# Output projections behind feed-forwards: the split of the last two inner tiles is issued one column tile earlier

## The chip, the cores and the metric

The kernel runs on one core of one Trainium2 chip. The metric is the device time of one execution in microseconds (us), here as the median over several runs.

## The reference, cut to what matters

The model is a two-layer decoder trunk on 256 tokens of width 1024. Each layer has a mixer (a short gated convolution in the first, an attention with three branches in the second) between two half-step feed-forwards, so that there are four feed-forwards in all:

```python
def swiglu_ffn(x, w_in, w_out):
    gate, up = jnp.split(x @ w_in, 2, axis=-1)
    return (jax.nn.silu(gate) * up) @ w_out
...
h = h + 0.5 * swiglu_ffn(rmsnorm(h, ffn1_norm[i]), ffn1_w_in[i], ffn1_w_out[i])
```

The inner width is 2816, which is 22 tiles of 128. The change concerns the last product, with `w_out`, of each of the four.

## The kernel before, in words

**Precision.** Every product is made of float32r matmuls on values that were split into a high half (a rounded copy) and a low half (what the rounding left). ScalarE (ACT) writes the high half, VectorE (DVE) subtracts to get the low half. For activations this is `split` (lines 361 to 363): one ACT cast on L362, then one DVE subtraction on L363, into one tile `act` of 128 x 512 whose left 256 columns are the high half and whose right 256 are the low half. A weight tile multiplies both halves with its own high part (128 x 512 matmuls, the function `wide`, L518), and its low part multiplies the high half alone (128 x 256 matmuls, the function `narrow`, L524).

**The weight stream.** `Stream` brings weights from HBM in blocks `ws` of 128 x 2048 (three buffers, issued on SyncE's queue, SP, L139). Half of a block is a unit: `high` casts it into `wh` on ACT (L166), `low` subtracts into `wl` on DVE (L183). At most six units are there at a time. When `narrow` has used the last tile of a unit, `W.done` lets the stream convert the unit that stands six further on. So the calls of `wide` and `narrow` also place casts on ACT's queue and subtractions on DVE's, in the order in which the program is written. Each engine works off its own instructions in that order; the order is not changed by a scheduler.

**The end of a feed-forward's first half.** `ffn_tokens` makes two inner tiles at a time. `turned` (L419) applies the SiLU and the gate and transposes, and sends the result to DRAM on SP (`turn`, L427); `placed` (L430) fetches it back in the layout that the output projection wants (`t<-turn`, L432); `halved` (L435) then calls `split` for the two tiles. For the last two inner tiles, `halved` is not called there but handed on as the function `rest`: two ACT casts and two DVE subtractions that are still to be issued.

**The output projection.** `out_proj` (L491) makes eight column tiles of 128 outputs. Each needs all 22 inner tiles. For the first four column tiles the work is cut in two. The first loop does inner tiles 0 to 17 of each of the four, 18 `wide` and then 18 `narrow` matmuls, in four PSUM banks. Then comes `rest()`. The second loop does inner tiles 18 to 21 of each of the four (four `wide`, four `narrow`) and hands the finished tile to `out_evac` (L473), which adds it to the residual on DVE (L475) and prepares the next norm. The weights of the first loop are nine units, 0 to 8; those of the second are units 9 and 10; column tiles five to eight follow from unit 11 on. In the first loop the third column tile uses up units 4 and 5, by which units 10 and 11 are converted; the fourth uses up units 6, 7 and 8, by which units 12, 13 and 14 are converted.

The calls with `rest` are the four behind feed-forwards: L702, L779, L1020 and L1362. The two other output projections, of the convolution and of the attention, don't take this way.

Of the kernel before, what the change touches and what calls it, by code (L numbers as in the profile page):

```python
# [69 lines left out]
def trunk(ctx, tc, A, out):  # L70
# [26 lines left out]
    def bank(shape=(P, 512)):  # L97
        return mk(shape, "a", 4, pool=ps)
# [250 lines left out]
    def a_pass(todo, last=7, mid=None):  # L349


        for o, u, xs, ks in todo:
            for k in ks:
                pe.matmul(o, u[0][:, k * P:(k + 1) * P], xs[k], start=(k == 0), stop=False)  # L354
        if mid is not None:
            mid()
        for o, u, xs, ks in todo:
            for k in ks:
                pe.matmul(o[:, :T], u[1][:, k * P:(k + 1) * P], xs[k][:, :T], start=False, stop=(k == last))  # L359
# [113 lines left out]
    def out_evac(o, c, factor, norm, short=False):  # L473
        for x in range(2):
            ve.scalar_tensor_tensor(out=h[c], in0=o[:, x * T:(x + 1) * T], scalar=factor, in1=h[c], op0=ALU.mult, op1=ALU.add)  # L475
        if not short:
            W.low()
            norm.tile(c)
            W.high()
            return  # L480
        norm.high(c)
        if c:
            norm.low(c - 1)
        if c < 5:
            W.low()
        W.high()
        norm.squares(c)
        if c == ND - 1:
            norm.low(c)

    def out_proj(lhs, factor, norm, final=False, rest=None):  # L491

        n, i, u = len(lhs), 0, None
        if rest is not None:
            n = NF
        head = []
        if n == 8:
            head = [(bank(), W.take()[0]) for _ in range(4)]
            cut = (7, 7, 7, 2)
            a_pass([(o, u, lhs, range(n)) for (o, u), n in zip(head, cut)])  # L500
        for c in range(len(head)):
            o, u = head[c]
            a_pass([(o, u, lhs, range(cut[c], 8))])
            W.done(1, False)
            out_evac(o, c, factor, norm, True)
        def tile():
            nonlocal i, u
            if i % 8 == 0:
                u, = W.take()
            q = slice(i % 8 * P, (i % 8 + 1) * P)  # L510
            i += 1
            return u[0][:, q], u[1][:, q], i % 8 == 0

        def wide(o, run, ks, last=None):
            for k in ks:
                while len(run) <= k:
                    run.append(tile())
                pe.matmul(o, run[k][0], lhs[k], start=(k == 0), stop=(k == last))  # L518

        def narrow(o, run, ks, last=None, free=True):  # L520
            for k in ks:
                while len(run) <= k:
                    run.append(tile())
                pe.matmul(o[:, :T], run[k][1], lhs[k][:, :T], start=False, stop=(k == last))  # L524
                if run[k][2] and free:
                    W.done(1, k < n - 1)

        c = len(head)
        if rest is not None:
            runs = [(bank(), []) for _ in range(4)]  # L530
            for o, run in runs:
                wide(o, run, range(n - 4))
                narrow(o, run, range(n - 4), n - 1)
            rest()
            for c, (o, run) in enumerate(runs):
                wide(o, run, range(n - 4, n))
                narrow(o, run, range(n - 4, n), n - 1)
                out_evac(o, c, factor, norm)
            c += 1
        while c < ND - final:  # L540
            o, run = bank(), []
            if n > 8 and c % 2 and c + 1 < ND - final:
                wide(o, run, range(n))
                o2, run2 = bank(), []
                wide(o2, run2, [0])
                narrow(o, run, range(n), n - 1)
                out_evac(o, c, factor, norm)
                narrow(o2, run2, range(n), free=False)
                wide(o2, run2, range(1, n), n - 1)
                for _ in range(sum(t[2] for t in run2)):  # L550
                    W.done(1, False)
                out_evac(o2, c + 1, factor, norm)
                W.pump()
                c += 2
                continue
            for ks in (range(n - 1), [n - 1]) if c == 0 else (range(n),):
                wide(o, run, ks)
                narrow(o, run, ks, n - 1)
            out_evac(o, c, factor, norm, n == 8)
            c += 1  # L560
        c -= 1
        if final:

            us = W.take((i + n + 7) // 8 - i // 8 - (i % 8 > 0))
            us = ([u] if i % 8 else []) + us
            w = [[us[(i % 8 + k) // 8][x][:, (i + k) % 8 * P:((i + k) % 8 + 1) * P] for x in range(2)] for k in range(n)]
            lo, hi = bank(), bank()
            for k in range(n):
                pe.matmul(lo[:, :T], w[k][0], lhs[k][:, T:], start=(k == 0), stop=(k == n - 1))
            ve.scalar_tensor_tensor(out=h[c + 1], in0=lo[:, :T], scalar=factor, in1=h[c + 1], op0=ALU.mult, op1=ALU.add)  # L570
            for q, o, ks in (slice(0, T), hi, range(n - 3)), (slice(0, P), hi, range(n - 3, n)), (slice(P, T), bank(), range(n - 3, n)):
                for k in ks:
                    pe.matmul(o[:, q], w[k][0], lhs[k][:, q], start=(k == ks[0] and q.start + k != n - 3), stop=False)
                    pe.matmul(o[:, q], w[k][1], lhs[k][:, q], start=False, stop=(k == n - 1))
                if k == n - 1:
                    z = q if o is not hi else slice(0, T)
                    ve.scalar_tensor_tensor(out=h[c + 1][:, z], in0=o[:, z], scalar=factor, in1=h[c + 1][:, z], op0=ALU.mult, op1=ALU.add)
                    norm.tile(c + 1, q)
        W.pump()
# [119 lines left out]
    hid, rest = ffn_tokens(xs, nm, n0=2, hid=hid, old=old)  # L699
    xs = new_xs()  # L700
    nm = Norm([(xs, G_MIX)])
    out_proj(hid, 0.5, nm, rest=rest)  # L702
    nm.halves()

# [40 lines left out]
    xs = new_xs()  # L745
    nm = Norm([(xs, G_FFN2)])
    out_proj(zs, 1.0, nm)
    bias = {}
    cbias = one([P, 8, 2, 2, 16], "cbias")
# [22 lines left out]
    hid, rest = ffn_tokens(xs, nm, bg=bias_bg, pre=lambda: list(tab))  # L772
# [4 lines left out]
    xkv = [xk_a[:, k] for k in range(4)] + [t2(dt=F32R) for _ in range(4)]  # L777
    nm = Norm([(xkv, G_KV), (xs, G_FFN1 + 8)])
    out_proj(hid, 0.5, nm, rest=rest)  # L779
    nm.halves()  # L780
    del hid
# [235 lines left out]
    hid, rest = ffn_tokens(xs, rc=rc, bg=bg)  # L1017
# [318 lines left out]
    for c in range(ND):  # L1336
        if c < 4:
            o = wo[c][0]
# [17 lines left out]
    hid, rest = ffn_tokens(xs, nm)  # L1356
# [93 lines left out]
```

## Time and profile before

| what | value |
|---|---|
| median of 3 runs | 964.2 us (963.87 to 965.33) |
| the profiled execution's own time | 964.24 us |
| its span in the trace | 962.5 us |
| busy: TensorE matmuls / weight loads | 951.4 us (99%) / 806.5 us (84%) |
| busy: VectorE / ScalarE / GpSimd | 662.3 / 538.7 / 136.5 us |
| granted TensorE clock | 1.00 |
| moved by DMA | 200.09 MB, 208 GB/s on the mean |

The span is what the trace covers, from the first to the last instruction; the execution's own time is 1.74 us longer. In rows of the trace, the number in front is the start in microseconds from the beginning of the span, the next one the duration; "x18" is a group of 18 instructions that follow each other, and the bracket behind a row is the idle time of the engine just before it and what ended that. The four output projections lie at about 127 to 190, 400 to 463, 623 to 687 and 896 to 957 us.

### The profile page before, as it was taken

How to read it: one execution, taken by the hardware profiler on the slowest of the kernel's cores; microseconds unless marked ns; L12 is line 12 of the kernel's file. 1: busy time of each engine (PE TensorE's matmuls, PEld its weight loads, DVE VectorE, ACT ScalarE, POOL GpSimd, SP SyncE). 2: the span in 40 equal slices, each digit the busy share in tenths (PEclk: the TensorE clock that was granted, in tenths of full speed). 3: DMA queues.
4: the chain of work that ended last, by engine and by line, in shares of the span. 5: the costliest groups of instructions: out<-in, count | busy, mean ns of one | idle time of the engine just before them, and what ended most of it. 6: DMA issues, size and time to landing. Idle time of an engine off the chain costs nothing.

```text
span 962.5 us, 13410 instructions
## 1 busy us (share of the span) xinstructions
PE 951.4 (99%) x4954; PEld 806.5 (84%) x4954; DVE 662.3 (69%) x1071; ACT 538.7 (56%) x903; POOL 136.5 (14%) x212
## 2 busy tenths in 40 slices
PE   9999999999999999999999999999999999999998
PEld 8888888888888888888888888888877888888888
DVE  6777667578896667656756676856579786677552
ACT  7755554455565555444647775644489774555430
POOL 2000000044520110001121031201137110000000
PEclk9999999999999999999999999999999999999999
DMA  8468885445546998764646886764511248877840
GB/s 308 176 219 264 277 258 191 190 176 208 179 170 242 262 280 259 229 239 175 218 163 206 266 254 239 250 240 161 197 46 46 89 175 267 277 221 243 276 160 21
DMA packets 127005, 200.09 MB, mean 208 GB/s; under 512 B 90539, under 2 KB 104875, under 8 KB 106332
## 3 DMA queue, kind: packets, MB, share of 16 engines
q1 hardware_dynamic: 126796, 198.97, 61.7%
q8 instruction: 39, 0.64, 0.3%
q10 hardware_dynamic: 144, 0.26, 0.1%
q14 instruction: 26, 0.21, 0.1%
HBM read 186.60 MB, written 12.09 MB: 206 GB/s over the span
## 4 chain that ended last, share of the span: by engine, by line
PE 98%; DVE 1%; DMA 1%; issue 0%; ACT 0%; SPq 0%; DVEq 0%
PE a L518 17%; PE mm L452 16%; PE mm L454 16%; PE mm L453 16%; PE a L524 9%; PE mm L354 4%; PE a L354 4%; PE mm L359 2%; PE a L359 2%; PE mm L1159 1%; PE mm L605 1%; PE a L1236 1%; PE a L795 1%; PE a L794 1%; PE a L796 1%; PE a L1204 1%
## 5 line engine op out<-in xcount | busy, mean ns | idle before, releaser
L183 DVE TENSOR_TENSOR wl<-ws,wh 128x1024 fp32r<-128x1024 f32 x318 | 390.5, 1253 | 191.8 <-ACT wh L166 155.0
L166 ACT CAST wh<-ws 128x1024 fp32r<-128x1024 f32 x318 | 325.9, 1047 | 190.7 <-DMA ws<-in_ffn_w_in_dram 84.9
L452 PE MATMUL mm<-wh,xs 128*128 128x512 f32 x672 | 262.6, 391 | 0.0
L454 PE MATMUL mm<-wl,xs 128*128 128x512 f32 x672 | 261.7, 389 | 0.0
L453 PE MATMUL mm<-wh,xs 128*128 128x512 f32 x672 | 261.5, 389 | 0.0
L518 PE MATMUL a<-act,wh 128*128 128x512 f32 x714 | 172.2, 392 | 6.4 <-DVE act L363 6.4
L518 PEld LDWEIGHTS a<-act,wh 128*128 128x128 f32 x714 | 131.2, 188 | 33.6 <-DVE act L363 8.3
L454 PEld LDWEIGHTS mm<-wl,xs 128*128 128x128 f32 x672 | 126.1, 188 | 27.0 <-DVE wl L183 0.5
L453 PEld LDWEIGHTS mm<-wh,xs 128*128 128x128 f32 x672 | 126.2, 188 | 25.7
L452 PEld LDWEIGHTS mm<-wh,xs 128*128 128x128 f32 x672 | 126.2, 188 | 25.7
L524 PEld LDWEIGHTS a<-act,wl 128*128 128x128 f32 x714 | 91.9, 191 | 3.6
L524 PE MATMUL a<-act,wl 128*128 128x256 f32 x714 | 93.0, 283 | 0.0
L315 POOL TENSOR_TENSOR sq<-sq,t 128x256 f32<-128x256 f32 x35 | 27.8, 795 | 382.8 <-ACT t L313 382.7
L423 ACT ACTIVATE t<-mm,rc 128x256 f32<-128x256 f32 x84 | 39.7, 473 | 56.6 <-DVE t L424 40.7
L298 ACT ACTIVATE xs<-base 128x256 fp32r<-128x256 f32 x48 | 24.0, 504 | 60.4 <-DVE base L475 50.7
L424 DVE SCALAR_TENSOR_TENSOR t<-mm,rc,t 128x256 f32<-128x256 f32 x84 | 40.5, 482 | 18.4 <-ACT t L423 15.2
L475 DVE SCALAR_TENSOR_TENSOR base<-a,base 128x256 f32<-128x256 f32 x78 | 32.8, 422 | 25.8 <-PE a L518 18.3
L362 ACT CAST act<-t 128x256 fp32r<-128x256 f32 x96 | 34.7, 404 | 24.8 <-DVE t L723 19.4
L363 DVE TENSOR_TENSOR act<-t,act 128x256 fp32r<-128x256 f32 x96 | 37.2, 424 | 5.9 <-ACT act L362 5.9
L425 DVE STREAM_TRANSPOSE t<-t 128x256 f32<-128x256 f32 x84 | 37.4, 446 | 3.0
L354 PE MATMUL mm<-xs,wh 128*128 128x512 f32 x144 | 34.7, 391 | 0.0
L302 DVE SCALAR_TENSOR_TENSOR xs<-base,xs 128x256 fp32r<-128x256 f32 x48 | 26.5, 556 | 9.5 <-ACT xs L298 9.4
(283 smaller groups left out, 900.5 us busy)
## 6 DMA issues: line engine op xcount, KB each, us to landing
ws<-in_ffn_w_in_dram SPq DMA_DIRECT2D x85, 1024.0 KB, 5.4
ws<-in_ffn_w_out_dram SPq DMA_DIRECT2D x44, 1024.0 KB, 5.6
ws<-in_conv_w_in_dram SPq DMA_DIRECT2D x12, 1024.0 KB, 4.6
turn<-t SPq DMA_DIRECT2D x42, 256.0 KB, 2.3
t<-turn SPq DMA_DIRECT2D x42, 256.0 KB, 7.2
ws<-in_w_kv_dram SPq DMA_DIRECT2D x6, 1024.0 KB, 4.8
ws<-in_conv_w_out_dram SPq DMA_DIRECT2D x4, 1024.0 KB, 4.7
ws<-in_attn_w_q_dram SPq DMA_DIRECT2D x4, 1024.0 KB, 4.8
```

What stands on the lines that cost most here:

```text
L166: ac.copy(h, src)
L183: ve.tensor_tensor(out=l, in0=src, in1=h.bitcast(F32), op=ALU.subtract)
L354: pe.matmul(o, u[0][:, k * P:(k + 1) * P], xs[k], start=(k == 0), stop=False)
L359: pe.matmul(o[:, :T], u[1][:, k * P:(k + 1) * P], xs[k][:, :T], start=False, stop=(k == last))
L423: ac.activation(s, o[:, tt, :T], AF.Silu, scale=rc[:, tt:tt + 1])
L424: ve.scalar_tensor_tensor(out=s, in0=o[:, tt, T:], scalar=rc[:, tt:tt + 1], in1=s, op0=ALU.mult, op1=ALU.mult)
L425: ve.transpose(tb[:, tt], s)
L452: pe.matmul(o[:, tt], sh, wh, start=(k == 0), stop=False)
L453: pe.matmul(o[:, tt], sl, wh, start=False, stop=False)
L454: pe.matmul(o[:, tt], sh, wl, start=False, stop=(k == 7))
L518: pe.matmul(o, run[k][0], lhs[k], start=(k == 0), stop=(k == last))
L524: pe.matmul(o[:, :T], run[k][1], lhs[k][:, :T], start=False, stop=(k == last))
```

## The change

In the first loop, the call of `rest()` moves from behind the fourth column tile to behind the third. The fourth column tile's 36 matmuls are issued behind it. Nothing else differs; one line is added, so that line numbers behind it are higher by one.

```diff
             runs = [(bank(), []) for _ in range(4)]
-            for o, run in runs:
+            for c, (o, run) in enumerate(runs):
                 wide(o, run, range(n - 4))
                 narrow(o, run, range(n - 4), n - 1)
-            rest()
+                if c == 2:
+                    rest()
             for c, (o, run) in enumerate(runs):
                 wide(o, run, range(n - 4, n))
                 narrow(o, run, range(n - 4, n), n - 1)
```

What this does to the queues is shown for the first output projection; in the other three the same instructions trade places. On DVE, `L363` is the subtraction of `split` for the last two inner tiles and `L183` that of the weights' low halves; `wl` is such a low half, `ws` the block that it comes from, `wh` the high half. The numbers behind the names count the tiles as the program makes them, so that those made behind the moved call are counted anew.

```order
 L183 TENSOR_TENSOR wl_1353<-ws_1277,wh_1351 128x1024
 L183 TENSOR_TENSOR wl_1367<-ws_1277,wh_1363 128x1024
-L183 TENSOR_TENSOR wl_1397<-ws_1321,wh_1395 128x1024
-L183 TENSOR_TENSOR wl_1411<-ws_1321,wh_1407 128x1024
-L183 TENSOR_TENSOR wl_1423<-ws_1365,wh_1421 128x1024
-L363 TENSOR_TENSOR act_1425<-t_231_1210,act_1425 128x256
-L363 TENSOR_TENSOR act_1428<-t_231_1210,act_1428 128x256
+L363 TENSOR_TENSOR act_1375<-t_231_1210,act_1375 128x256
+L363 TENSOR_TENSOR act_1378<-t_231_1210,act_1378 128x256
+L183 TENSOR_TENSOR wl_1403<-ws_1321,wh_1401 128x1024
+L183 TENSOR_TENSOR wl_1417<-ws_1321,wh_1413 128x1024
+L183 TENSOR_TENSOR wl_1429<-ws_1365,wh_1427 128x1024
```

The two subtractions of `split` have moved ahead of the three weight subtractions of units 12, 13 and 14. The first two rows, units 10 and 11, stay in front of both.

On ACT, at the same place, `L362` is the cast of `split` and `L166` the cast of the weights' high halves.

```order
 L166 CAST wh_1351<-ws_1277 128x1024
 L166 CAST wh_1363<-ws_1277 128x1024
-L166 CAST wh_1395<-ws_1321 128x1024
-L166 CAST wh_1407<-ws_1321 128x1024
-L166 CAST wh_1421<-ws_1365 128x1024
-L362 CAST act_1425<-t_231_1210 128x256
-L362 CAST act_1428<-t_231_1210 128x256
+L362 CAST act_1375<-t_231_1210 128x256
+L362 CAST act_1378<-t_231_1210 128x256
+L166 CAST wh_1401<-ws_1321 128x1024
+L166 CAST wh_1413<-ws_1321 128x1024
+L166 CAST wh_1427<-ws_1365 128x1024
```

The two casts of `split` have likewise moved ahead of the three weight casts. The order of the matmuls on TensorE, of the transfers on SP and of what GpSimd does is the same in both kernels.

## Prediction

> **What bounds the kernel now.** I read the page's busy times and its chain first, then the waits of TensorE (PE), then the timelines of PE, ACT, DVE and SP around the first output projection, then the same rows at the other three. First the page's head and the chain's shares by engine; then PE's waits (line that waited, who ended it, us in total, times, longest):
>
> ```profile
> span 962.5 us, 13410 instructions
> PE 951.4 (99%) x4954; PEld 806.5 (84%) x4954; DVE 662.3 (69%) x1071; ACT 538.7 (56%) x903; POOL 136.5 (14%) x212
> PE 98%; DVE 1%; DMA 1%; issue 0%; ACT 0%; SPq 0%; DVEq 0%
> ```
>
> ```profile
> PE a L518 <- DVE act L363: 6.4, 4, 1.6
> PE a L254 <- DVE ones L229: 1.1, 1, 1.1
> PE mm L605 <- ACT xs L298: 0.4, 1, 0.4
> PE a L1204 <- ACT xs L1214: 0.4, 1, 0.4
> ```
>
> The kernel is bound by PE almost throughout, so a microsecond in which PE stands still is a microsecond of the time. The largest of its waits, 6.4 us in four pieces, is for L363, the subtraction that the change moves. PE's timeline shows one of them, in the first output projection:
>
> ```profile
> 151.62 0.63 PE L518 MATMUL a<-act,wh 128*128 128x512 f32 x2
> 153.84 0.84 PE L518 MATMUL a<-act,wh 128*128 128x512 f32 x2 [1.59 <-DVE act L363]
> 154.52 0.64 PE L524 MATMUL a<-act,wl 128*128 128x256 f32 x4
> 154.99 1.08 PE L518 MATMUL a<-act,wh 128*128 128x512 f32 x4
> 155.91 0.64 PE L524 MATMUL a<-act,wl 128*128 128x256 f32 x4
> 156.38 1.09 PE L518 MATMUL a<-act,wh 128*128 128x512 f32 x4
> 157.78 1.09 PE L518 MATMUL a<-act,wh 128*128 128x512 f32 x4
> ```
>
> At 151.62 the second loop begins: two matmuls with inner tiles 18 and 19, then PE stands until inner tile 20 is split. The other three column tiles of this loop run without a wait, one each 1.39 to 1.40 us (154.99, 156.38, 157.78).
>
> Why L363 is late is read from ACT's timeline (first fence) and DVE's (second) at the same place:
>
> ```profile
> 143.45 2.00 ACT L166 CAST wh<-ws 128x1024 fp32r<-128x1024 f32 x2 [0.48 <-DMA ws<-in_ffn_w_out_dram]
> 146.02 1.05 ACT L166 CAST wh<-ws 128x1024 fp32r<-128x1024 f32 x1 [0.58 <-PE a L518]
> 147.85 1.05 ACT L166 CAST wh<-ws 128x1024 fp32r<-128x1024 f32 x1 [0.77 <-PE a L518]
> 149.66 1.05 ACT L166 CAST wh<-ws 128x1024 fp32r<-128x1024 f32 x1 [0.76 <-PE a L518]
> 150.62 0.71 ACT L362 CAST act<-t 128x256 fp32r<-128x256 f32 x2
> ```
>
> ```profile
> 142.05 4.84 DVE L183 TENSOR_TENSOR wl<-ws,wh 128x1024 fp32r<-128x1024 f32 x4 [5.07 <-ACT wh L166]
> 149.95 3.50 DVE L183 TENSOR_TENSOR wl<-ws,wh 128x1024 fp32r<-128x1024 f32 x3 [3.06 <-PE a L524]
> 153.37 0.76 DVE L363 TENSOR_TENSOR act<-t,act 128x256 fp32r<-128x256 f32 x2
> 155.19 0.89 DVE L475 SCALAR_TENSOR_TENSOR base<-a,base 128x256 f32<-128x256 f32 x2 [1.07 <-PE a L524]
> ```
>
> The three weight casts (units 12 to 14) each wait until PE has used up an old unit in the fourth column tile, and the casts of `split` are queued behind them. On DVE it is worse: the three weight subtractions can't begin before 149.95, when the fourth column tile's `narrow` part frees the first buffer, then take 3.50 us, and only at 153.37 comes L363. What PE wants at once stands behind three conversions that nobody wants soon.
>
> **The change part by part.** Four instructions move, two on ACT and two on DVE, at each of four places; nothing is added, and no transfer, SP entry or GpSimd instruction changes its place.
>
> *What goes.* Start to start, the first column tile of the second loop takes 154.99 - 151.62 = 3.37 us, where one without a wait takes 1.395. The other three places read the same:
>
> ```profile
> 424.73 0.63 PE L518 MATMUL a<-act,wh 128*128 128x512 f32 x2
> 428.10 1.08 PE L518 MATMUL a<-act,wh 128*128 128x512 f32 x4
> 648.27 0.63 PE L518 MATMUL a<-act,wh 128*128 128x512 f32 x2
> 651.63 1.08 PE L518 MATMUL a<-act,wh 128*128 128x512 f32 x4
> 920.47 0.63 PE L518 MATMUL a<-act,wh 128*128 128x512 f32 x2
> 923.83 1.08 PE L518 MATMUL a<-act,wh 128*128 128x512 f32 x4
> ```
>
> That is 3.37, 3.36 and 3.36 us. Together 13.46 us, of which 4 x 1.395 = 5.58 remain: 7.88 us can go. The row of PE's waits says less, 6.4 us. I take the starts, because the durations there are too long to be occupancy: two matmuls are shown as 0.63 us, though four follow each other in 155.91 - 154.99 = 0.92 us; idle time counted from such ends is too small by the difference, about 0.17 us, and the 0.68 us from 153.84 to 154.52 for two matmuls, instead of 0.46, is the second one's wait for the second subtraction. [...]
>
> *The casts on ACT.* They now stand behind units 10 and 11, which end at 143.45 + 2.00 = 145.45. Their input must have landed. The first row here is the last fetch on SP, the second the time from issue to landing of the transfers of `turn` in the whole run, 42 each way (shortest, median, longest):
>
> ```profile
> 134.11 0.60 SPq L432 DMA_DIRECT2D t<-turn  x1
> DMA to landing us min/median/max: 2.1/2.8/9.8
> ```
>
> Issued at 134.11, even the longest landing, 9.8 us, would have it there by 143.9, so they run from 145.45 to 146.16. The next weight cast, at 146.02, slips by 0.14 us, and the idle 0.77 us ahead of the one behind takes that up. At the other places the gap is wide:
>
> ```profile
> 419.14 1.05 ACT L166 CAST wh<-ws 128x1024 fp32r<-128x1024 f32 x1 [2.93 <-PE a L518]
> 642.68 1.05 ACT L166 CAST wh<-ws 128x1024 fp32r<-128x1024 f32 x1 [2.59 <-PE a L518]
> 914.88 1.05 ACT L166 CAST wh<-ws 128x1024 fp32r<-128x1024 f32 x1 [2.92 <-PE a L518]
> ```
>
> 0.71 us fits into each. Cost: nothing. Were that cover gone, three weight casts would slip by 0.71 us, and their units are not multiplied before the fifth column tile.
>
> *The subtractions on DVE.* They stand behind the four weight subtractions that end at 142.05 + 4.84 = 146.89, and take 0.76 us, to 147.65. DVE is idle there until 149.95 anyway, 3.06 us by its row. At the other places the idle time ahead of the same three subtractions is:
>
> ```profile
> 423.07 3.50 DVE L183 TENSOR_TENSOR wl<-ws,wh 128x1024 fp32r<-128x1024 f32 x3 [3.66 <-issue]
> 646.61 3.50 DVE L183 TENSOR_TENSOR wl<-ws,wh 128x1024 fp32r<-128x1024 f32 x3 [3.66 <-issue]
> 918.80 3.50 DVE L183 TENSOR_TENSOR wl<-ws,wh 128x1024 fp32r<-128x1024 f32 x3 [3.66 <-issue]
> ```
>
> Cost: nothing. Inner tiles 20 and 21 are then split 4.4 us before PE asks for them, at about 151.62 + 2 x 0.23 = 152.08.
>
> *What is late next.* The weights of the second loop, units 9 and 10, are converted by 146.89. The first tile's evacuation, L475, finds its product at 155.19 - 1.97 = 153.22 but DVE in the weight subtractions until 149.95 + 3.50 = 153.45: 0.23 us late, with 1.08 us idle before it today and a bank that PE wants again three column tiles later, 4.2 us on. Nothing on PE's path is charged.
>
> The sum against the profiled execution: 964.24 - 7.88 = 956.36 us. That execution is at the median of the runs shown (964.2), so the forecast is **956.3 us**. The expected difference, 0.8%, stands well above what a measurement of this kernel can tell from no change, about 0.2% or 1.9 us.
>
> **The rivals.**
>
> *The idle time shown is all there is.* If the durations are right, 6.4 us go: 957.8 us. Against it, the pace of the next column tiles.
>
> *The wait comes back later.* PE reaches each next piece 1.97 us earlier, and the weights might not. What the DMA engines do around the first place is in these stretches (length, busy PE, PEld, DVE, ACT, POOL with counts, clock, DMA share, GB/s):
>
> ```profile
> 146.00:151.00 5.00, 5.00 (x29) 4.36 (x29) 1.94 (x2) 3.45 (x5) 0.00 (x0) 1.00 0.94 385
> 151.00:156.00 5.00, 3.41 (x20) 2.61 (x19) 3.90 (x7) 0.33 (x2) 0.00 (x0) 1.00 0.55 197
> 156.00:161.00 5.00, 5.00 (x29) 4.34 (x28) 3.77 (x9) 3.40 (x7) 0.95 (x2) 1.00 0.05 21
> ```
>
> For it: a DMA share of 0.94 just before the place. Against it: the share then falls to 0.55 and 0.05, and the waits quoted above hold none of PE for a weight tile. The conversions of units 12 to 14 wait for PE to free buffers (ACT's and DVE's rows above), so they come no later than today. If half is given back all the same: 964.24 - 3.94 = 960.3 us; if all, 964.2.
>
> *The change doesn't do what it says.* PE's wait could hang on the landing of the fetched tiles and only be put down to L363; then the time stays 964.2. Against it: L363 starts directly behind the weight subtractions, at 153.37, with no idle time of its own.
>
> *Slower: a late landing blocks the queues.* The moved casts now stand ahead of three weight casts, so a fetch that lands late holds those up too. [...] The trace agrees: the casts at 150.62 and the subtractions at 153.37 start only when the conversions ahead are done. From 9.8 us, the longest landing, nothing yet happens. PE is worse off than today only if the splits end after 153.37 + 0.76 = 154.13; ACT and DVE need about 0.35 + 0.76 = 1.1 us for them, so the point is a landing at 153.0, 18.9 us after issue, nearly twice the longest. At 20.4 us after issue, PE would lose 1.5 us more than today at each place: 964.24 + 6 = 970.2 us.
>
> **How the numbers follow.** Chances: 0.82 for the forecast, 0.07 for the shown idle time alone, 0.06 for giving back (0.04 of it still faster by over 0.2%, 0.02 not), 0.02 for a change that does nothing, 0.03 for slower. So faster 0.82 + 0.07 + 0.04 = 0.93, same 0.04, slower 0.03. The range takes in the first two cases. Low: 956.3 less 0.8, the two small waits of 0.4 us that might shrink, 955.5. High: 957.8 plus 1.1, the distance of the slowest run shown (965.33) from the median, 958.9.
>
> **What would show it.** Right: the row of PE waiting for L363 is gone; the second loop's first column tile takes 1.4 us like the others; the two casts start within 0.2 us of the end of units 10 and 11 on ACT, the two subtractions behind the weight subtractions there, over 4 us before PE needs them; each later stage begins earlier by 1.97 us for each place passed, the fourth place by 5.9 us. Wrong: a new wait of PE for `wl` or `wh` behind one of the places, a cast on L362 that waits for `t<-turn`, or a span shortened by less than 6 us.

## The result and the profile after

| | before | changed |
|---|---|---|
| median | 964.5 us (6 runs, 963.87 to 965.33) | 956.56 us (6 runs, 956.06 to 957.04) |
| the profiled execution's own time | 964.24 us | 956.48 us |
| its span | 962.5 us | 954.7 us |

The ratio is 0.9918, with a 95% interval of 0.9905 to 0.993. The forecast was 956.3 us, in a range of 955.5 to 958.9.

The page of the changed kernel, its head and its chain by engine, and then all waits of TensorE (PE):

```profile
span 954.7 us, 13410 instructions
PE 950.0 (100%) x4954; PEld 807.2 (85%) x4954; DVE 661.3 (69%) x1071; ACT 538.2 (56%) x903; POOL 135.8 (14%) x212
...
PE 99%; DMA 1%; ACT 0%; SPq 0%; issue 0%; DVE 0%
```

```profile
PE a L254 <- DVE ones L229: 1.1, 1, 1.1
PE a L1205 <- ACT xs L1215: 0.4, 1, 0.4
PE mm L606 <- ACT xs L298: 0.4, 1, 0.4
```

The wait for the split is gone, and no wait has come in its place. PE's timeline at the first output projection:

```profile
151.66 1.09 PE L518 MATMUL a<-act,wh 128*128 128x512 f32 x4
152.59 0.63 PE L524 MATMUL a<-act,wl 128*128 128x256 f32 x4
153.06 1.09 PE L518 MATMUL a<-act,wh 128*128 128x512 f32 x4
...
154.47 1.09 PE L518 MATMUL a<-act,wh 128*128 128x512 f32 x4
...
155.87 1.09 PE L518 MATMUL a<-act,wh 128*128 128x512 f32 x4
```

The second loop's four `wide` matmuls of the first column tile now stand in one group, and this column tile takes 1.40 us like the others. ACT (first fence) and DVE (second) there:

```profile
145.09 2.00 ACT L166 CAST wh<-ws 128x1024 fp32r<-128x1024 f32 x2 [0.42 <-DMA ws<-in_ffn_w_out_dram]
147.00 0.71 ACT L362 CAST act<-t 128x256 fp32r<-128x256 f32 x2
147.61 2.00 ACT L166 CAST wh<-ws 128x1024 fp32r<-128x1024 f32 x2
152.28 1.05 ACT L166 CAST wh<-ws 128x1024 fp32r<-128x1024 f32 x1 [2.67 <-DMA ws<-in_ffn_w_out_dram]
```

```profile
143.76 4.77 DVE L183 TENSOR_TENSOR wl<-ws,wh 128x1024 fp32r<-128x1024 f32 x4 [5.88 <-ACT wh L166]
148.45 0.75 DVE L363 TENSOR_TENSOR act<-t,act 128x256 fp32r<-128x256 f32 x2
150.00 2.36 DVE L183 TENSOR_TENSOR wl<-ws,wh 128x1024 fp32r<-128x1024 f32 x2 [0.80 <-ACT wh L166]
153.36 1.23 DVE L183 TENSOR_TENSOR wl<-ws,wh 128x1024 fp32r<-128x1024 f32 x1 [1.00 <-ACT wh L166]
154.50 0.88 DVE L475 SCALAR_TENSOR_TENSOR base<-a,base 128x256 f32<-128x256 f32 x2
```

The casts and the subtractions of the split follow units 10 and 11 directly, in the gaps that were idle. The last subtraction ends at 149.20. At the other places DVE's rows of the split are these (first fence), and PE's first and second column tile of the second loop start so (second fence):

```profile
417.41 0.76 DVE L363 TENSOR_TENSOR act<-t,act 128x256 fp32r<-128x256 f32 x2
639.00 0.75 DVE L363 TENSOR_TENSOR act<-t,act 128x256 fp32r<-128x256 f32 x2
909.25 0.75 DVE L363 TENSOR_TENSOR act<-t,act 128x256 fp32r<-128x256 f32 x2
```

```profile
422.82 1.09 PE L518 MATMUL a<-act,wh 128*128 128x512 f32 x4
424.22 1.09 PE L518 MATMUL a<-act,wh 128*128 128x512 f32 x4
644.41 1.09 PE L518 MATMUL a<-act,wh 128*128 128x512 f32 x4
645.81 1.09 PE L518 MATMUL a<-act,wh 128*128 128x512 f32 x4
914.66 1.09 PE L518 MATMUL a<-act,wh 128*128 128x512 f32 x4
916.06 1.09 PE L518 MATMUL a<-act,wh 128*128 128x512 f32 x4
```

Each takes 1.40 us, so 3.37 - 1.40 = 1.97 us went at the first two places and 1.96 us at the last two, 7.86 us together. The second loops start 1.91, 3.86 and 5.81 us earlier than before at places two, three and four (the first one 0.04 us later, 151.66 against 151.62), which is 1.95 us for each place passed, and the span is 7.8 us shorter. Nothing is given back between the places.

### The profile page after: what moved, and what is told of

Its sections match the earlier page's. It is cut to its first block, busy times and chain, and to the rows that moved or that the text cites. A ratio compares the mean times of both kernels' runs of the same rounds, so it can differ in the third digit from the quotient of the medians.

```text
span 954.7 us, 13410 instructions
## 1 busy us (share of the span) xinstructions
PE 950.0 (100%) x4954; PEld 807.2 (85%) x4954; DVE 661.3 (69%) x1071; ACT 538.2 (56%) x903; POOL 135.8 (14%) x212
## 4 chain that ended last, share of the span: by engine, by line
PE 99%; DMA 1%; ACT 0%; SPq 0%; issue 0%; DVE 0%
PE a L518 17%; PE mm L452 16%; PE mm L454 16%; PE mm L453 16%; PE a L524 9%; PE mm L354 4%; PE a L354 4%; PE mm L359 2%; PE a L359 2%; PE mm L1160 1%; PE mm L606 1%; PE a L1237 1%; PE a L796 1%; PE a L795 1%; PE a L797 1%; PE a L1205 1%
## 5 line engine op out<-in xcount | busy, mean ns | idle before, releaser
L183 DVE TENSOR_TENSOR wl<-ws,wh 128x1024 fp32r<-128x1024 f32 x318 | 390.4, 1252 | 190.2 <-ACT wh L166 161.9
L166 ACT CAST wh<-ws 128x1024 fp32r<-128x1024 f32 x318 | 325.6, 1047 | 191.4 <-DMA ws<-in_ffn_w_in_dram 84.9
L362 ACT CAST act<-t 128x256 fp32r<-128x256 f32 x96 | 34.7, 404 | 24.1 <-DVE t L724 19.4
L475 DVE SCALAR_TENSOR_TENSOR base<-a,base 128x256 f32<-128x256 f32 x78 | 32.7, 421 | 21.4 <-PE a L518 18.2
L363 DVE TENSOR_TENSOR act<-t,act 128x256 fp32r<-128x256 f32 x96 | 37.2, 423 | 5.7 <-ACT act L362 5.7
```

Source lines behind the costliest of these rows:

```text
L166: ac.copy(h, src)
L183: ve.tensor_tensor(out=l, in0=src, in1=h.bitcast(F32), op=ALU.subtract)
```

## The experiments

The theory: PE stood because L363 was queued on DVE behind three weight subtractions. The rivals that were left: the casts' place on ACT, a gain given back further on, and a landing that blocks the queues. The kernel before was timed beside each group of runs. A diff is against the changed kernel where it is not said otherwise.

**Only the casts early.** The two ACT casts are issued behind the third column tile, the two DVE subtractions behind the fourth.

```diff
+        def casts():
+            for f in range(2):
+                hd = act()
+                ac.copy(hd[:, :T], way[:, f])
+                hid.append(hd)
+        def lows():
+            for f, hd in enumerate(hid[-2:]):
+                ve.tensor_tensor(out=hd[:, T:], in0=way[:, f], in1=hd[:, :T].bitcast(F32), op=ALU.subtract)
-        return hid, lambda: halved(way)
+        return hid, (casts, lows)
...
                 if c == 2:
-                    rest()
+                    rest[0]()
+            rest[1]()
```

> Only half of the change: in all four output projections the two ACT casts of the split are issued behind the third column tile, the two DVE subtractions behind the fourth, as before. My theory is that TensorE waits for the subtractions because they stand behind three weight subtractions on DVE: then nothing is gained, 964.5 us, and TensorE still waits 1.6 us four times for the subtraction of the split. The rival, that the casts' place on ACT is what costs: 956.6 us, the whole gain.

Measured: 967.19 us against 965.03, ratio 1.0025 (1.0011 to 1.0038). Its ACT and DVE at the first place, and PE's waits for the subtraction (here on L479):

```profile
146.67 0.71 ACT L474 CAST act<-t 128x256 fp32r<-128x256 f32 x2
```

```profile
150.25 3.50 DVE L183 TENSOR_TENSOR wl<-ws,wh 128x1024 fp32r<-128x1024 f32 x3 [2.03 <-PE a L534]
153.66 0.75 DVE L479 TENSOR_TENSOR act<-t,act 128x256 fp32r<-128x256 f32 x2
```

```profile
PE a L528 <- DVE act L479: 6.7, 4, 1.7
```

The casts are done at 147.4 and nothing is gained: the subtractions still come behind the 3.50 us. So ACT's order alone does not remove the wait. But the time is 2.7 us over what I expected. PE at the third place shows part of it, and behind it the stretches (length, busy PE, PEld, DVE, ACT, POOL with counts, granted clock, DMA share, GB/s):

```profile
651.06 0.80 PE L528 MATMUL a<-act,wh 128*128 128x512 f32 x2 [1.68 <-DVE act L479]
651.70 0.83 PE L534 MATMUL a<-act,wl 128*128 128x256 f32 x4
652.33 1.91 PE L528 MATMUL a<-act,wh 128*128 128x512 f32 x4
```

```profile
650.00:655.00 5.00, 3.94 (x15) 3.39 (x16) 2.58 (x6) 0.81 (x2) 0.00 (x0) 0.70 0.65 213
655.00:660.00 5.00, 5.00 (x27) 4.22 (x27) 4.22 (x8) 2.58 (x5) 1.53 (x2) 0.96 0.00 0
```

Behind this stall four `wide` matmuls take 1.91 us instead of 1.09, and the granted clock falls short by 0.30 x 5 + 0.04 x 5 = 1.7 us: 3.4 us at half clock, if it was halved (the run with one added subtraction shows 0.50 over a whole stretch, last section). All ten executions of this kernel had a mean granted clock of 0.998 or less. That led to the runs with longer stalls below.

**Only the subtractions early.** On ACT the order of before, on DVE that of the change: the fourth column tile's three weight subtractions are held back behind the split (the diff is against the kernel before).

```diff
-            for o, run in runs:
+            for c, (o, run) in enumerate(runs):
                 wide(o, run, range(n - 4))
-                narrow(o, run, range(n - 4), n - 1)
+                narrow(o, run, range(n - 4), n - 1, c < 3)
+            for _ in range(3):
+                W.done(1, False)
+                W.high()
             rest()
+            for _ in range(3):
+                W.low()
```

> The other half: the casts of the split stand behind the three weight casts on ACT as before, but on DVE its two subtractions stand ahead of the three weight subtractions. Theory (DVE's order costs): the casts end at about 151.3 in the first place, the subtractions at 151.85, TensorE asks for them at 152.1, so nearly the whole gain, 956.6 to 957.0 us; up to 2 us more if ACT's third weight cast waits for its block from HBM at one place, as it did in the first place of the changed kernel. Rival (ACT's order costs): 964.5 us.

Measured: 956.81 us against 965.03, ratio 0.9916 (0.9891 to 0.994), the whole gain within the spread of the executions. One of its four took 960.30 us, at a mean clock of 0.998; it was not the profiled one, so where it lost the time is not shown. At the first place of the profiled one ACT, DVE and PE:

```profile
150.97 0.71 ACT L362 CAST act<-t 128x256 fp32r<-128x256 f32 x2
```

```profile
151.40 0.76 DVE L363 TENSOR_TENSOR act<-t,act 128x256 fp32r<-128x256 f32 x2 [3.67 <-ACT act L362]
152.08 3.49 DVE L183 TENSOR_TENSOR wl<-ws,wh 128x1024 fp32r<-128x1024 f32 x3
```

```profile
151.24 1.48 PE L518 MATMUL a<-act,wh 128*128 128x512 f32 x4
...
153.03 1.09 PE L518 MATMUL a<-act,wh 128*128 128x512 f32 x4
```

The casts stand as late as in the kernel before, the split ends at 152.16, and PE loses only 1.79 - 1.40 = 0.39 us there and nothing at the other three. With the run before it this settles the cause: DVE's order.

**In two of the four places.** The change in the first two output projections alone (`if c == (3, 2)[early]`, with `early=True` at those two calls).

> The change in the first two of the four output projections alone. Theory (each place is worth its own stall of 1.97 us and nothing is given back later): 964.5 - 2 x 1.97 = 960.6 us, with two waits of 1.6 us left. Rival (part of what an early place gains is given back further on, or one place carries the most): clearly off the middle, 958 or 963 us.

Measured: 960.05 us against 965.03, ratio 0.9944 (0.9926 to 0.9962). PE's waits:

```profile
PE a L518 <- DVE act L363: 3.2, 2, 1.6
```

The span is 958.5 us, 4.0 us below that of the kernel before. Each place is worth its own stall. (One of the five executions, at a mean clock of 0.998, took 961.88 us.)

**Behind the first column tile.** `if c == 0:` instead of `if c == 2:`.

> The split is issued earlier still, behind the first column tile instead of the third, so that its casts stand ahead of seven weight casts. Theory (any place is the same in which the split is done before TensorE asks and the fetched tiles have landed): 956.6 us as with the change, within 0.5 us. Rival one (more lead is worth more): below 956 us. Rival two (ACT and DVE are held up by the landing, and the weights behind them come late): above 957.5 us, with a wait of ACT for the fetched tiles.

Measured: 956.64 us against 965.03, ratio 0.9906 (0.9888 to 0.9924). ACT at the first place:

```profile
139.36 0.71 ACT L362 CAST act<-t 128x256 fp32r<-128x256 f32 x2 [3.11 <-DMA t<-turn]
```

ACT is now held up by the landing for 3.11 us, and the time is that of the change. Part of the second rival, the held-up engine, is there; its cost is not.

**Half of the stall.** Two of the three weight subtractions ahead of the split, one behind (the edit of "only the subtractions early", with the first two `W.low()` ahead of `rest()`).

> A stall in between: the split stands ahead of the last of the three weight subtractions on DVE, behind the first two, and behind all three weight casts on ACT. Theory (TensorE's wait is the DVE queue ahead of the split): 1.14 us of the 1.97 us go at each place, 964.5 - 4.6 = 959.9 us, with waits of about 0.8 us, or some tenths less, and a clock of 1.00. Rival (the wait is for something else that ends by chance at that time, such as ACT's casts): 964.5 or 956.6 us.

Measured: 960.53 us against 964.71, ratio 0.9961 (0.9946 to 0.9976). PE at the second place:

```profile
424.51 0.63 PE L518 MATMUL a<-act,wh 128*128 128x512 f32 x2
425.60 0.83 PE L518 MATMUL a<-act,wh 128*128 128x512 f32 x2 [0.46 <-DVE act L363]
...
426.73 1.09 PE L518 MATMUL a<-act,wh 128*128 128x512 f32 x4
```

2.22 - 1.40 = 0.82 us are lost, where 0.83 was worked out: PE's wait follows the number of weight subtractions ahead of L363 one by one. Its first place still took 3.28 us, because there the split waited for its own casts on ACT, behind a weight cast that came late (151.75); so the time is 0.6 us over.

**Longer stalls.** In the kernel before, the last weight subtraction is repeated ahead of the split, twice (as in the diff) or once.

```diff
             ve.tensor_tensor(out=l, in0=src, in1=h.bitcast(F32), op=ALU.subtract)
+            self.again = lambda: ve.tensor_tensor(out=l, in0=src, in1=h.bitcast(F32), op=ALU.subtract)
...
+            W.again()
+            W.again()
             rest()
```

> The kernel before with a longer stall: the last of the three weight subtractions is made twice more (same operands, same result) ahead of the split on DVE. A subtraction in a row of three takes (3.50 - 1.22) / 2 = 1.14 us, so the split comes 2.28 us later at each of four places. Theory one, a stall costs its own length and nothing else: 964.5 + 9.1 = 973.6 us, granted clock 1.00. Theory two, from the run with the casts alone, whose record holds a stretch of 3.41 us at half clock right behind one of its stalls: a long enough stall also costs such a stretch, up to 1.7 us a place, so up to 980.4 us, mean clock about 0.993.

> The kernel before with a stall longer by one weight subtraction instead of two: 1.14 us more at each of four places. A stall at its own length alone: 964.5 + 4.6 = 969.1 us at a clock of 1.00. With the half-clock stretches that the run with two more subtractions showed at every place: 1 to 2 us more at most places, 972 to 976 us, and a mean clock of 0.993 to 0.996.

Measured: with two 982.89 us against 964.71, ratio 1.0191 (1.0176 to 1.0206), mean clock 0.988 to 0.991; with one 975.15 us against 965.76, ratio 1.0086 (1.0062 to 1.0109), clock 0.991 to 0.998. With one, PE at the second place, and the stretches there:

```profile
430.01 0.63 PE L519 MATMUL a<-act,wh 128*128 128x512 f32 x2
433.50 0.84 PE L519 MATMUL a<-act,wh 128*128 128x512 f32 x2 [2.85 <-DVE act L364]
...
434.65 1.91 PE L519 MATMUL a<-act,wh 128*128 128x512 f32 x4
...
438.99 1.09 PE L519 MATMUL a<-act,wh 128*128 128x512 f32 x4
```

```profile
430.00:435.00 5.00, 2.15 (x11) 1.50 (x10) 3.85 (x6) 0.00 (x0) 0.00 (x0) 0.96 0.63 218
435.00:440.00 5.00, 5.00 (x21) 4.19 (x20) 3.56 (x9) 2.84 (x7) 0.33 (x1) 0.70 0.00 2
```

From 430.01 to the start of the fourth column tile, 438.99, go 8.98 us; three column tiles without a stall are 4.20. Of the 4.78 us lost, 1.97 are the old stall and 1.14 the added subtraction, and 1.67 come from the half clock behind it, again 1.7 / 0.5 = 3.4 us long. So theory one, a stall costs its own length alone, falls. The run with two subtractions went 2.5 us past theory two as well: I had allowed one such stretch a place, but in the profiled execution the granted clock was 0.63 and 0.69 in the two stretches of 5 us from 155 to 165 us, at its first place, and 0.64 and 0.67 from 660 to 670 us, at its third. That is 3.4 and 3.45 us short, two such stretches at each; over the whole execution 0.012 x 981.8 = 11.8 us were short, by estimate seven of them. A second part is no matter of the clock: its first place stood for 5.50 us and the others for 4.11, because a weight cast on ACT waited 1.95 us for its block and held up the subtractions behind it. In the run with one it was the same, 5.40 us against 2.85. And the half clock does not follow every stall of 2.85 us: one of that run's four executions took 972.20 us at a mean clock of 0.998, a shortfall of about 0.002 x 970 = 1.9 us, one such stretch in four places.

**The fetch issued late.** SP issues the last `t<-turn` at the call of `rest()` behind the third column tile; the second kernel does the same, with the split in the old place.

```diff
                     way = turned(o)
-                    if g == last:
-                        way = placed(way)
...
-        return hid, lambda: halved(way)
+        return hid, lambda: halved(placed(way))
```

> The changed kernel with the last fetch issued late: SP issues it at the call behind the third column tile, after four more weight blocks, at about 145 instead of 134 us in the first place. This tries the rival that a late landing blocks the queues. If it lands 4 us later, at 149, the splits are done at about 150.1, before TensorE asks at 152.1: 956.6 us, although the three weight casts behind it slip by 3 us. If it lands at the longest time seen, 9.8 us, at 155, TensorE waits 4 us at each place: 964.5 + 4 x 2 = 972.5 us, slower than before. With the theory that only the end of the split counts, the time follows the landing, 1 us for each us behind 151.0.

> The same late fetch, with the split behind the fourth column tile as in the kernel before. If the fetch lands before 152.3, when the three weight subtractions are nearly done, nothing changes from the kernel before: 964.5 us. Against the run with the late fetch and the early split this shows whether the early place is worse than the late one when the landing is late: only if that run is the slower of the two does the blocking of the queues decide.

Measured: 956.48 us against 964.71 with the split early, ratio 0.9918 (0.9903 to 0.9933); 964.08 us with the split in the old place, ratio 0.9992 (0.9983 to 1.0002). ACT of the first:

```profile
148.03 0.71 ACT L362 CAST act<-t 128x256 fp32r<-128x256 f32 x2 [4.46 <-DMA t<-turn]
```

ACT stands 4.46 us for the landing, the weight casts behind it too, and it costs nothing. The landing was still in time, so I made it later: a copy of 1 MB from HBM to HBM that nobody reads is issued on SP just ahead of the fetch, in both kernels.

```diff
...
+        def fetched():
+            sy.dma_start(mk([P, CHUNK], "junk", 1, pool=dr), A["ffn2_w_out"][1][:, :CHUNK])
+            return placed(way)
...
```

> The changed kernel with the last fetch later still: SP issues a copy of 1 MB from HBM to HBM, whose result nobody reads, just ahead of it (four copies in all). In the run with the late fetch it landed about 5.5 us after its issue at 142.3; with the copy I expect 153 to 155. If the end of the split alone counts, TensorE then stands about 3 us instead of 1.8 at each place, 964.5 + 4 x 1.3 = 970 us, up to 977 with half-clock stretches, and as long as the same fetch with the split in the old place. If the blocking of ACT and DVE costs by itself (the three weight conversions held up behind the landing), this kernel is slower than that one by 2 us or more.

> The same copy and late fetch, with the split behind the fourth column tile as in the kernel before. If the end of the split alone counts: 970 to 977 us, within 1 us of the run with the split early, since both wait for the same landing. If the queues' blocking counts: faster than that run by 2 us or more, since here the weight conversions don't stand behind the landing.

Measured: 957.79 us against 965.76 with the split early, ratio 0.9916 (0.9901 to 0.9931); 964.54 us in the old place, ratio 0.9987 (0.9978 to 0.9996). That the second ratio is below one is no gain of that kernel: 7 of the 13 executions of the kernel before in this group had a mean clock of 0.998, on which more below. Both miss what I expected for the landing, which came at about 152 and not at 153 to 155. In the old place the cast waited 1.60 us for it and was still done before DVE had finished the three weight subtractions at 153.5. ACT and PE of the first kernel at the first place:

```profile
152.07 0.71 ACT L362 CAST act<-t 128x256 fp32r<-128x256 f32 x2 [8.43 <-DMA t<-turn]
```

```profile
151.56 0.63 PE L520 MATMUL a<-act,wh 128*128 128x512 f32 x2
152.99 0.83 PE L520 MATMUL a<-act,wh 128*128 128x512 f32 x2 [0.80 <-DVE act L363]
...
154.13 1.09 PE L520 MATMUL a<-act,wh 128*128 128x512 f32 x4
```

ACT is held up for 8.43 us, and PE loses 2.57 - 1.40 = 1.17 us, still less than the 1.97 us of the old order. At the other places it loses nothing. The early place is the faster one even then: what counts here is the end of the split, and the weights behind it have time. A landing late enough to make the early place the worse one was not reached.

## Why the prediction was right

*What goes.* The stall is worth its start-to-start difference, 7.86 us by the traces (7.88 forecast) and 7.8 us of the span, not the 6.4 us of the waits' row. On this the pace of the neighbouring column tiles, 1.395 us from start to start, was the right measure; counting idle time would have forecast 957.8 us. One reading inside the sum is only half right: of the 0.22 us that the prediction puts down to the wait for the second subtraction, 0.11 lie ahead of that matmul and 0.11 behind it (starts at 153.84, 154.18 and 154.52). The start-to-start difference holds both, so the sum is not changed.

*The casts and the subtractions cost nothing.* Shown by the rows after and by the runs of one half each. The forecast lead of 4.4 us at the first place was 152.1 - 149.2 = 2.9 us in this execution, since the weight blocks landed later and units 10 and 11 were converted later; at the second place it is 423.3 - 418.2 = 5.1 us. I had not allowed for weights that land later: 2.9 us is the smallest margin of the change, and the sign "over 4 us before PE needs them" failed at this place. The three weight casts behind the split did not slip by 0.14 us: two followed it at once and the third waited 2.67 us for its block. That made the first evacuation (L475, 154.50) 1.4 us late behind PE's 153.06, not 0.23 us. PE shows no wait for it either.

*The chain to the end.* Each place passed brings the next one 1.95 us forward; the run with two places has half of the gain. Giving back, 0.06, did not happen.

*The rivals.* That L363 was only put down as the releaser falls with the two half changes. The slower rival had the blocking right, up to 8.43 us of ACT, and its point right as far as it could be tried: PE loses only what the split ends too late. The latest landing that was tried, at 152.07, came 0.9 us short of the 153.0 where the prediction put the point; what happens beyond it is not shown.

*What the prediction did not have.* The stall has a second price that its own length does not show, the half clock behind it, which the profiled execution of before did not contain (granted clock 1.000). So the kernel before is sometimes slower than that profile says, and the forecast of the difference holds for executions without it. In that the forecast had luck: worked out from an execution of 966.7 us, the middle of those with the half clock, the same subtraction would have given 966.7 - 7.9 = 958.8 us, 2.2 us over what was measured.

## What to carry to other kernels

Where an engine waits for a short conversion, look at what is queued ahead of it on the converting engine: here the split's two subtractions started only when three weight subtractions of 3.50 us ahead of them were done, and a few rows moved past this work, which had slack, were worth the whole stall, 1.97 us at a place. Count such a stall from start to start against a neighbour that does not wait, and try the two halves of a moved step apart, since here one half carried everything. The early place cost nothing here as long as the split was done before it was needed and the work behind it was not due, even where its engine stood for the input (4.46 us); leave margin for weight blocks that land late.

## What the runs showed of the hardware that I had not expected

A stall of about 2 us can cost more than itself. Behind the wait at the third place of the kernel with the casts alone (1.68 us by the trace's row) the granted clock fell short by 1.7 us, which is 3.4 us at half clock, and such a stretch costs nearly as much as the stall itself (1.67 us where it was counted above, beside 1.97). The half is read directly at the first place of the kernel with one added subtraction, where PE's wait ended at 157.29 (0.50; the columns as above):

```profile
155.00:160.00 5.00, 2.71 (x8) 2.40 (x9) 3.10 (x6) 0.00 (x0) 0.00 (x0) 0.50 0.52 213
```

The length of a stall alone does not tell whether the half clock follows. With the casts alone, the second two matmuls of the second loop started 2.31 us behind the first two at the first place (151.92 and 154.23) and at the third (648.75 and 651.06) alike. Behind the first place the next four `wide` matmuls took 1.09 us, behind the third 1.91. In the profiled execution of the kernel before it was 2.22 us at each place, and the granted clock of the stretches around all four was 1.00. What else decides is not shown.

In the kernel before, 13 of its 40 executions beside the experiments had a mean granted clock of 0.998, by estimate 0.002 x 965 = 1.9 us short, about one such stretch in four places. They took 965.7 to 968.07 us (middle value 966.73); the other 27, at 0.999 or 1.000, took 963.66 to 965.76 us. The two kernels with a late fetch and the split in the old place, which stall alike, had 0.998 in one of 20. Of the 14 executions of the three kernels in which no place stalls (the change, the split behind the first column tile, the fetch issued late) none was below 0.999, and they lie between 955.88 and 957.04 us.
